# A sliding-window copy on one core: three DMA rings in place of two, new packet sizes, and eleven batches staged in place of twelve

## The chip, the cores and the metric

The kernel runs on one core of a Trainium2 chip. The metric is the device time of one execution in microseconds (us). MB and GB are powers of ten, as in the profile; KB is 1,024 bytes.

## The reference

```
batch, length, dim = (32, 4096, 256); window_size = 64; stride = 32      # float32
n_windows = (length - window_size) // stride + 1                         # 127
for i in range(n_windows):
    start = i * stride
    result[:, i] = x[:, start:start + window_size].copy()
```

Nothing is calculated. Each window is 64 rows of 256 floats, 64 KB without a gap, and the next one begins 32 rows further on. So x falls into blocks of 32 rows (32 KB), 128 to a batch. Window w is blocks w and w+1, and each inner block is written twice: as the second half of one window and as the first half of the next. One batch of x is 4.194 MB; its 127 windows are 8.323 MB of output.

## The kernel before

No compute engine takes part. The work is DMA: an engine's queue issues a transfer, the hardware cuts it into packets, and 16 DMA engines move them. Every issuing queue has a ring of waiting packets on each of the 16. SP feeds q1 and ACT feeds q10 (the bytes in the profile tell which is which). There are two ways for a batch, and the 32 batches are shared out between them:

- **Copied** (20 batches, issued by SP, `copy`, L93). Three transfers go straight from x to the output in memory, of 80, 32 and 15 windows, in packets of 16, 32 and 16 KB (`COPY_PARTS`, L16). The DMA engines move 8.323 MB a batch; memory is read and written for all of it.
- **Staged** (the 12 odd batches 1 to 23, issued by ACT, `load` L75 and `store` L83). One load puts the batch into a tile `xb` of 128 partitions, a block in each (4.194 MB). Two stores write the tile to the first halves of the windows and to the second halves (4.194 MB each). All in packets of 16 KB. The DMA engines move 12.58 MB a batch, and memory is read for one third of that and written for two.

Five tiles are in use in turn (`BUFS`). ACT's program is load 0, load 1, stores 0, load 2, stores 1, and so on (L142 to L148); a store waits for its load (L88), and the load of a tile's next turn waits for both stores of its last (L79). All of these stand one behind the other in one ring.

A store of all 128 blocks writes one block too many at each end: half a window into the batch before and half a window into the batch behind. Those neighbours are copied batches, and they are put right in one of two ways. Most are copied only when the stores that spill into them have landed (L134 to L137; `_order`, L102, places such a batch in SP's list far enough behind). The four of `EARLY` are copied at the very start, and SP writes their spilt halves once more at the end: seven small transfers of 32 KB each, the fringes, in packets of 2 KB (`half`, L46; L152 to L158). ACT waits for the `EARLY` copies before the first store that spills into one (L145 to L147). At the end SP waits for everything and clears 12 semaphores one by one (L159 to L163).

Of the kernel before, what the change touches and what calls it, by code (L numbers as in the profile page):

```python
# [1 line left out]

# [4 lines left out]


STAGED = tuple(range(1, 24, 2))
BUFS = 5  # L10

EARLY = (18, 20, 22, 24)

BLOCK_PARTS = 2

COPY_PARTS = ((80, 4), (32, 2), (15, 4))  # L16


class _Geometry:


    def __init__(self, x, out, W, S):
        self.B, self.L, self.D = x.shape
        self.x, self.out = x, out
        self.n_win = (self.L - W) // S + 1
        self.n_blk = self.L // S
        self.blk = S * self.D
        self.win = W * self.D
        assert W == 2 * S and self.n_blk == self.n_win + 1 == 128

    def src(self, b, block, dims):

        at = (b * self.n_blk + block) * self.blk
        return bass.AP(self.x.tensor, self.x.offset + at, dims)

    def dst(self, b, half, dims):

        at = b * self.n_win * self.win + half * self.blk
        return bass.AP(self.out.tensor, self.out.offset + at, dims)

    def rows(self, b, w0, n):

        s, d = [[self.blk, n], [1, self.win]], [[self.win, n], [1, self.win]]
        return self.dst(b, 2 * w0, d), self.src(b, w0, s)

    def half(self, b, half, block):  # L46

        dims = [[self.blk // 16, 16], [1, self.blk // 16]]
        return self.dst(b, half, dims), self.src(b, block, dims)


class _Kernel:
    def __init__(self, nc, g, tiles):
        self.nc, self.g, self.tiles = nc, g, tiles
        self.loaded = [nc.alloc_semaphore(f"loaded{i}") for i in range(len(tiles))]
        self.stored = [nc.alloc_semaphore(f"stored{i}") for i in range(len(tiles))]
        self.copied = nc.alloc_semaphore("copied")
        self.early = nc.alloc_semaphore("early")
        self.count = {}

    def start(self, engine, out, in_, sem, parts=1):
        engine.dma_start(out=out, in_=in_, max_dma_last_dim=65536 // parts).then_inc(sem, 16)
        self.count[id(sem)] = self.count.get(id(sem), 0) + 16

    def all_of(self, engine, sem):
        engine.wait_ge(sem, self.count[id(sem)])

    def slot(self, n):
        return divmod(n, len(self.tiles))

    def after_store(self, engine, n):
        turn, i = self.slot(n)
        engine.wait_ge(self.stored[i], 32 * (turn + 1))

    def load(self, n):  # L75

        g, (_, i) = self.g, self.slot(n)
        if n >= len(self.tiles):
            self.after_store(self.nc.scalar, n - len(self.tiles))  # L79
        src = g.src(STAGED[n], 0, [[g.blk, g.n_blk], [1, g.blk]])  # L80
        self.start(self.nc.scalar, self.tiles[i][:, :], src, self.loaded[i], 2 * BLOCK_PARTS)

    def store(self, n):  # L83

        g, (turn, i) = self.g, self.slot(n)
        self.nc.scalar.wait_ge(self.loaded[i], 16 * (turn + 1))  # L88
        for half in (0, -1):
            dst = g.dst(STAGED[n], half, [[g.win, g.n_blk], [1, g.blk]])  # L90
            self.start(self.nc.scalar, dst, self.tiles[i][:, :], self.stored[i], 2 * BLOCK_PARTS)

    def copy(self, b, sem):  # L93

        w = 0
        for rows, parts in COPY_PARTS:
            self.start(self.nc.sync, *self.g.rows(b, w, rows), sem, parts)
            w += rows
        assert w == self.g.n_win


def _order(B):  # L102


    near = {b for s in STAGED for b in (s - 1, s + 1)}
    order = list(EARLY) + [b for b in range(B) if b not in near and b not in STAGED]
    tied = sorted(near - set(EARLY))
    n = len(order) + len(tied)
    for b in tied:
        behind = max(STAGED.index(s) for s in (b - 1, b + 1) if s in STAGED)  # L110
        order.insert(-(-(2 * behind + 5) * n // (2 * len(STAGED))), b)
    return order


@with_exitstack
def kernel(
    ctx: ExitStack,
    tc: tile.TileContext,
    x: bass.AP,
    window_size: bass.AP,  # L120
    stride: bass.AP,
    out: bass.AP,
):
    nc = tc.nc
    W, S = int(window_size), int(stride)
    g = _Geometry(x, out, W, S)
    assert 0 not in STAGED and g.B - 1 not in STAGED
    pool = ctx.enter_context(tc.tile_pool(name="blocks", bufs=1))
    tiles = [pool.tile([g.n_blk, g.blk], x.dtype, name=f"xb{i}") for i in range(BUFS)]

    with tc.tile_critical():
        k = _Kernel(nc, g, tiles)
        for b in _order(g.B):
            if b not in EARLY:  # L134
                for s in (b - 1, b + 1):
                    if s in STAGED:
                        k.after_store(nc.sync, STAGED.index(s))  # L137
            k.copy(b, k.early if b in EARLY else k.copied)
        k.load(0)
        waited = False  # L140
        last = len(STAGED) - 1
        for n, s in enumerate(STAGED):  # L142
            if n < last:
                k.load(n + 1)
            if not waited and (s - 1 in EARLY or s + 1 in EARLY):  # L145
                k.all_of(nc.scalar, k.early)
                waited = True  # L147
            k.store(n)  # L148


        k.all_of(nc.sync, k.early)
        for n, s in enumerate(STAGED):  # L152
            if s - 1 in EARLY or s + 1 in EARLY:
                k.after_store(nc.sync, n)
            if s - 1 in EARLY:
                k.start(nc.sync, *g.half(s - 1, 2 * g.n_win - 1, g.n_blk - 1), k.copied)
            if s + 1 in EARLY:
                k.start(nc.sync, *g.half(s + 1, 0, 0), k.copied)  # L158
        for n in range(len(STAGED)):  # L159
            k.after_store(nc.sync, n)  # L160
        k.all_of(nc.sync, k.copied)
        for sem in [*k.loaded, *k.stored, k.copied, k.early]:
            nc.sync.sem_clear(sem)  # L163


# [1 line left out]
_INS = ['x', 'window_size', 'stride']  # L167
_OUTS = [((32, 127, 64, 256), 'float32')]

_NUMBERS = {'window_size': 64, 'stride': 32}  # L170


# [26 lines left out]
```

## Time and profile before

| | |
|---|---|
| median of 3 runs | 763.64 us (762.43 to 763.97) |
| the profiled execution's own time | 768.4 us |
| its span, first to last instruction | 766.6 us |
| moved by the DMA engines | 317.70 MB in 19,837 packets, mean 414 GB/s |
| q1 (SP's ring): the copies and fringes | 10,044 packets, 166.70 MB |
| q10 (ACT's ring): loads and stores | 9,792 packets, 151.00 MB |
| memory read and written | 217.02 and 267.35 MB, 632 GB/s over the span |
| issue to landing, median | 114.8 us (80-window copy), 123.2 us (load), 84.6 us (store) |

How to read it: no engine row has any work but four tiny fills by GpSimd at the start, so the chain of waits between compute engines is empty and tells nothing. What matters is the row of DMA shares over 40 slices (the mean busy share of the 16 DMA engines, in tenths), the row of GB/s below it, and the DMA queues with their packets, bytes and share of 16 engines' time. The same can be asked for any stretch of the span. An issue's time to landing holds its wait in the ring behind all that was issued ahead of it.

### The profile page before, as it was taken

The numbers are of one execution on the slowest core, as the hardware profiler recorded it, in microseconds if no ns is written. First come the engines' busy times: TensorE is split into PE (matmuls) and PEld (weight loads), VectorE is DVE, ScalarE is ACT, GpSimd is POOL, SyncE is SP. The second block draws the span as 40 slices with busy tenths as digits, with TensorE's granted clock in tenths as the row PEclk, the third lists the DMA queues.
The fourth block names the chain that finished last, engine by engine and source line by source line (L and its number), as shares of the span: only waits on it lengthen the run. The fifth ranks groups of instructions, "written<-read, shape, count | busy, mean of one in ns | idle before, by whom it ended". The sixth has DMA issues, their size and how long they took to land. (4 is left out here: it accounts for less than half of the span.)

```text
span 766.6 us, 180 instructions
## 1 busy us (share of the span) xinstructions
POOL 0.2 (0%) x4
## 2 busy tenths in 40 slices
POOL 0000000000000000000000000000000000000000
DMA  8999999999999999999999999999999999999996
GB/s 371 425 410 421 405 428 431 408 411 427 423 415 421 431 415 425 432 408 416 427 420 417 431 420 420 423 428 410 414 427 419 422 428 418 417 428 421 420 406 237
DMA packets 19837, 317.70 MB, mean 414 GB/s; under 512 B 1628, under 2 KB 1628, under 8 KB 1740
## 3 DMA queue, kind: packets, MB, share of 16 engines
q1 hardware_dynamic: 10044, 166.70, 51.9%
q10 hardware_dynamic: 9792, 151.00, 47.3%
q14 instruction: 1, 0.01, 0.0%
HBM read 217.02 MB, written 267.35 MB: 632 GB/s over the span
## 5 line engine op out<-in xcount | busy, mean ns | idle before, releaser
L180 POOL MEMSET const-bfloat16-1.0<- 128x1 bf16 x1 | 0.1, 102 | 0.0
L180 POOL MEMSET const-uint8-127<- 128x1 uint8 x1 | 0.1, 102 | 0.0
L180 POOL MEMSET const-float32-0.0<- 128x1 f32 x1 | 0.1, 99 | 0.2 <-issue 0.2
L180 POOL MEMSET const-float32-1.0<- 128x1 f32 x1 | 0.1, 99 | 0.0
## 6 DMA issues: line engine op xcount, KB each, us to landing
out_dram<-in_x_dram SPq DMA_DIRECT2D x20, 5120.0 KB, 114.8
out_dram<-xb ACTq DMA_DIRECT2D x24, 4096.0 KB, 84.6
xb<-in_x_dram ACTq DMA_DIRECT2D x12, 4096.0 KB, 123.2
out_dram<-in_x_dram SPq DMA_DIRECT2D x20, 2048.0 KB, 116.7
out_dram<-in_x_dram SPq DMA_DIRECT2D x20, 960.0 KB, 97.7
out_dram<-in_x_dram SPq DMA_DIRECT2D x7, 32.0 KB, 48.3
```

The source lines that it names most:

```text
L180: nc = _bacc.Bacc("TRN2", target_bir_lowering=False, num_devices=1)
```

## The change

Eleven odd batches (1 to 21) are staged and 21 are copied; `EARLY` becomes 16, 18, 20, 22. GpSimd issues the loads from load 1 on, on a ring of its own, in packets of 8 KB; ACT keeps load 0 (now without a cut, 32 KB) and issues all stores in packets of 16 KB; SP issues the copies as 112 and 15 windows in packets of 32 KB. The last staged batch is stored in three pieces: partitions 0 to 31, 96 to 127, and then 32 to 95. The first two write what spills into the neighbours and have a semaphore `fringe`, so that the last two fringe transfers wait for those pieces alone. Load 0 has a semaphore `first` of its own. At the end GpSimd, not SP, waits for all semaphores, resets its DMA state and clears the semaphores as one range. There are seven fringe transfers as before.

```diff
-STAGED = tuple(range(1, 24, 2))
+STAGED = tuple(range(1, 22, 2))
-EARLY = (18, 20, 22, 24)
-BLOCK_PARTS = 2
-COPY_PARTS = ((80, 4), (32, 2), (15, 4))
+EARLY = (16, 18, 20, 22)
+LOAD_PACKET = 8192
+STORE_PACKET = 16384
+COPIES = ((112, 2), (15, 2))
+LAST = ((0, 32), (96, 32), (32, 64))
...
     def load(self, n):
         if n >= len(self.tiles):
-            self.after_store(self.nc.scalar, n - len(self.tiles))
+            self.after_store(self.nc.gpsimd, n - len(self.tiles))
         src = g.src(STAGED[n], 0, [[g.blk, g.n_blk], [1, g.blk]])
-        self.start(self.nc.scalar, self.tiles[i][:, :], src, self.loaded[i], 2 * BLOCK_PARTS)
+        if n == 0:
+            self.start(self.nc.scalar, self.tiles[i][:, :], src, self.first)
+        else:
+            self.start(self.nc.gpsimd, self.tiles[i][:, :], src, self.loaded[i], LOAD_PACKET)
...
+    def store(self, n, p0, rows, sem=None):
...
         for half in (0, -1):
-            dst = g.dst(STAGED[n], half, [[g.win, g.n_blk], [1, g.blk]])
-            self.start(self.nc.scalar, dst, self.tiles[i][:, :], self.stored[i], 2 * BLOCK_PARTS)
+            dst = g.dst(STAGED[n], 2 * p0 + half, [[g.win, rows], [1, g.blk]])
+            src = self.tiles[i][p0 : p0 + rows, :]
+            self.start(self.nc.scalar, dst, src, sem or self.stored[i], STORE_PACKET)
...
+        k.load(0)
         for b in _order(g.B):
...
-        k.load(0)
+        for n in range(1, len(STAGED)):
+            k.load(n)
...
-            if n < last:
-                k.load(n + 1)
...
-            k.store(n)
+            if n < last:
+                k.store(n, 0, g.n_blk)
+            else:
+                for p0, rows in LAST:
+                    alone = p0 > 0 and p0 + rows < g.n_blk
+                    k.store(n, p0, rows, None if alone else k.fringe)
...
-            if s - 1 in EARLY or s + 1 in EARLY:
+            if n == last:
+                k.all_of(nc.sync, k.fringe)
+            elif s - 1 in EARLY or s + 1 in EARLY:
                 k.after_store(nc.sync, n)
...
-        for n in range(len(STAGED)):
-            k.after_store(nc.sync, n)
-        k.all_of(nc.sync, k.copied)
-        for sem in [*k.loaded, *k.stored, k.copied, k.early]:
-            nc.sync.sem_clear(sem)
+        sems = [*k.loaded, *k.stored, k.first, k.early, k.copied, k.fringe]
+        for sem in sems:
+            k.all_of(nc.gpsimd, sem)
+        nc.gpsimd.dma_reset()
+        used = sorted(sem.num for sem in sems)
+        nc.gpsimd.sem_clear(range(used[0], used[-1] + 1))
```

## The prediction

> **What bounds the kernel now.** I read the page's DMA rows first, since no compute engine works, then the queues, then single stretches of the span.
>
> ```profile
> DMA  8999999999999999999999999999999999999996
> q1 hardware_dynamic: 10044, 166.70, 51.9%
> q10 hardware_dynamic: 9792, 151.00, 47.3%
> HBM read 217.02 MB, written 267.35 MB: 632 GB/s over the span
> ```
>
> All slices but the first and last are full, and the two rings' shares add up to 99.2% of the time of 16 engines. There is no wait to remove: the time is bytes times what a byte costs a DMA engine. From the rows, per MB on one engine: q1 0.519 x 766.6 us x 16 / 166.70 = 38.2 us, q10 0.473 x 766.6 x 16 / 151.00 = 38.4 us. Straight copies and staged traffic cost the same per byte moved, though a copied byte uses memory twice.
>
> Next, stretches by what ACT's ring is doing. The load that was issued at 44 us is served from 83.5 to 104.6, two stores follow, and so on; three such groups:
>
> ```profile
> 83.50:104.60 21.10, 0.00 (x0) 1.00 1.00 409
> 104.70:125.30 20.60, 0.00 (x0) 1.00 1.01 430
> 125.30:145.70 20.40, 0.00 (x0) 1.00 1.01 427
> 333.80:355.90 22.10, 0.00 (x0) 1.00 1.01 407
> 356.00:376.70 20.70, 0.00 (x0) 1.00 1.02 433
> 376.80:397.20 20.40, 0.00 (x0) 1.00 0.99 418
> 521.80:543.40 21.60, 0.00 (x0) 1.00 1.00 407
> 543.50:563.80 20.30, 0.00 (x0) 1.00 1.00 425
> 563.90:585.00 21.10, 0.00 (x0) 1.00 1.01 421
> ```
>
> Each row ends with the DMA share and GB/s. In the load stretches (first of each three, mean 408) packets take longer than in the store stretches (mean 426), with the engines just as busy: when both rings read memory, something is 4% short. That matters below.
>
> Then how two rings share an engine, from the queues of 31 to 35 us, where most copy packets were the 32 KB ones:
>
> ```profile
> q1 hardware_dynamic: 32, 1.05, 60.7%
> q10 hardware_dynamic: 34, 0.56, 32.5%
> ```
>
> Almost as many packets each, but twice the bytes in q1: the rings take turns packet by packet, so packet sizes set the shares. Last, the end:
>
> ```profile
> 720.00:750.00 30.00, 0.00 (x0) 1.00 0.95 406
> 750.00:753.00 3.00, 0.00 (x0) 1.00 0.91 355
> 753.00:755.00 2.00, 0.00 (x0) 1.00 1.04 393
> 755.00:757.00 2.00, 0.00 (x0) 1.00 0.78 294
> 757.00:759.00 2.00, 0.00 (x0) 1.00 0.78 241
> 759.00:761.00 2.00, 0.00 (x0) 1.00 0.51 198
> 761.00:763.00 2.00, 0.00 (x0) 1.00 0.14 54
> ```
>
> From 720 us the share is 0.95, about 15/16: one engine is out of work. That is the 15-window copy, which can be dealt to 15 engines only. So 15 engines set the end. From 755 us they fall out one by one.
>
> **The change part by part.**
>
> *One staged batch becomes a copied one.* On each of the 15 busy engines a copied batch is 8 windows, 512 KB; a staged one is 256 KB in and 512 KB out. Before: 20 x 512 + 12 x 768 = 19,456 KB. After: 21 x 512 + 11 x 768 = 19,200 KB. The 256 KB (0.262 MB) that go cost 0.262 x 38.3 = **-10.0 us**. All of it is on the path, since nothing else sets the end.
>
> *Packet sizes.* In the trace's packet records the medians are 611 ns for 16 KB and 1,213 ns for 32 KB, so 2 x 611 - 1,213 = 9 ns a packet beyond its bytes; the 4-byte semaphore packets take 9 ns too. Per busy engine before: 20 x (20 + 4 + 4) + 12 x 48 = 1,136 packets. After: copies 21 x 16 = 336, stores 11 x 32 = 352, loads 8 + 10 x 32 = 328, in all 1,016. 120 x 9 ns = **-1.1 us**. An 8 KB packet isn't in the rings of before; by this fit it takes 310 ns. Ends: no saving (0), or this one; what a GpSimd ring could add is a rival below.
>
> *The third ring.* Loads leave ACT's ring. In a full round of turns an engine takes 32 KB of copy, 16 of store, 8 of load: 57, 29 and 14%, where the bytes are 56, 29 and 15%. Load 0 in 32 KB turns ends after 8 rounds of 72 KB, about 22 us at 38.3 us per MB; before, it took 20. Stores of a batch then need 32 rounds, and so does the next load, which has a head start of about 9: ACT's ring doesn't run dry. Loads need tiles: load n waits for stores n-5, four batches back, and queued behind that wait on GpSimd are only later loads, needed later still. SP's list: the last tied batch (14) is 20th of 21 and starts after 19 x 16 rounds, some 650 us; stores 7, for which it waits, land at about 23 + 8 x 68 = 570 us. Issue to landing is 115 us in before, so ahead of that wait SP's ring still holds two copies. The fill of all 16 engines is the cover of all this; if a ring runs dry, the others take its turns, and the cost is only an uneven end.
>
> What the mix does to the rate is the unknown. Before, loads come in lumps of a third of the time with reads only in q10; after, one byte in seven is a load, always. Ends: all of it as in the store stretches, 426 against a mean of 419 over full windows, 1.6% of 750 = -12 us; all as in the load stretches, 408, +2.7% = +20 us. Bytes read from memory as a part of bytes moved are 217.0/317.7 = 68% before, and (174.8 + 46.1 + 0.2)/313.4 = 71% after; it is 100% in the load stretches and about 53% in the others. Linear between those rows, 3 points of 47 times 18 GB/s is 1 GB/s, 0.2%: **+1.5 us**.
>
> *The end.* From 750 us 3.4 MB are left; at 406 GB/s that is 8.5 us, and it took about 13.5. So the end loses 5 us to engines that finish apart and to copies left alone. After, copies run out about 25 store packets an engine (15 us) before the stores, by the count of rounds; the last two fringes wait only for the outer pieces and so are issued before the inner one (16 packets, 10 us) is done. What ends late is then stores, whose stretches were the fast ones. But engines can still finish apart. Ends 0 and -5; I take **-2 us**.
>
> *First and last microseconds.* Load 0 is still ACT's first; only 2 to 6 us was thin (365 GB/s), so at most 1 us either way: 0. SP's 12 clears took 0.7 us (764.9 to 765.6) and become one; GpSimd's reset isn't in the trace. Ends -0.7 and, by the whole stretch behind the last packet, +2.9 once more: 0, as near a clear.
>
> Sum: -10.0 - 1.1 + 1.5 - 2 = -11.6 us. The profiled execution would go from 768.4 to 756.8; it lies 4.8 us over the median of the runs, and I take the same difference from that: 763.64 - 11.6 = **752.0 us**.
>
> A rule that speaks against a third ring: the Trainium skill, "DMA: Bandwidth & Descriptors", section "Rules for kernel authors", says that spreading DMAs over SP, ACT and GpSimd brings no bandwidth, as they use the same 16 engines. The shares of 0.99 to 1.01 above agree that none is idle; by the rule alone the sum is bytes and packets, -11.1 us. The same page, "Queues, rings and completion order", has an engine drain typically 9 to 17 descriptors of a ring before it turns to the next. The 32 against 34 packets above say one at a time for these two rings; if the rule held for GpSimd's ring, loads would take 72 to 136 KB a turn until the tiles are full, which is the fourth rival.
>
> **The rivals.**
>
> 1. *The lumps go* (faster still). Packets are stretched only when everything reads at once. For: 408 against 426. Against: store stretches aren't even themselves (418 to 433). 752 - 1.5 - 12 = **738.5**.
> 2. *The mix is as slow as a load stretch throughout* (slower than before). For: memory traffic per moved byte rises from 484.4/317.7 = 1.52 to 488.5/313.4 = 1.56, and loads are never absent till near the end. Against: 71% of reads is nearer 53 than 100. 752 - 1.5 + 20 = **770.5**. It decides from a full rate of 413 GB/s in the middle (419 less 1.5%).
> 3. *GpSimd's packets are dear* (slower). Its 8 KB load packets are 320 an engine, each with an unknown addition. Low end 0; far end the seven 8 KB packets of the instruction queue, which took 500 ns on average, 190 over the fit: +61 us, **813**. It decides from 11.6 / 0.32 = 36 ns a packet. Those seven are fetches of another kind; the rings' own 9 ns a packet is nearer.
> 4. *The shares don't come out*: loads run ahead, and copies or stores are left alone for long at the end. Bytes are as counted; the end keeps its loss and takes it once more: 752 + 2 + 5 = **759**.
>
> **How the numbers follow.** Forecast (746 to 758) 0.53; rival 1 0.18; rival 4 0.08; rival 2 0.12, of which 0.04 ends within 0.2%; rival 3 0.09, of which 0.01 does. 0.2% (1.5 us) is about what a measurement of this kernel can tell from no change. Faster 0.79, within 0.05, slower 0.16. The range goes down to rival 1's end, 739, and up to 768, which leaves out most of rivals 2 and 3, under 2 in 10.
>
> **What would show it.** A third queue with 42 MB (10 loads), ACT's with about 96, SP's with 175; 313.4 MB in all. Right: 418 to 420 GB/s level through the middle, no dips to 408. Rival 1: over 424. Rival 2: under 413 with the share at 1.0. Rival 3: the third queue's share of time far over its 13% of bytes. Rival 4: a ring that ends over 30 us before the others. The forecast is wrong if the DMA share falls below 0.98 in mid-span.

## The result, and the profile after

The changed kernel takes 753.76 us (median of 6 runs, 751.49 to 756.93) against 763.50 us of the kernel before (median of 6, 761.43 to 764.13). The ratio is 0.9883, with a 95% interval from 0.9856 to 0.9910: faster by 1.2%; by the medians it is 9.7 us. The profiled execution took 756.93 us, the longest of the six, with a span of 755.1. The profiled execution of before took 768.4, 4.8 us above the median, so a second trace of before (e11) stands beside it below.

From the page of the changed kernel, the DMA queues and the memory row:

```profile
q1 hardware_dynamic: 6209, 175.02, 54.8%
q10 hardware_dynamic: 6192, 96.47, 30.4%
q0 software_dynamic: 5280, 41.94, 13.6%
HBM read 221.15 MB, written 267.29 MB: 647 GB/s over the span
```

A third queue, q0, is GpSimd's, with the ten loads. Its share of time, 13.6%, is about its share of the bytes, 41.94 of 313.43 MB or 13.4%. The shares still add up to 98.8%: the engines are as full as before, with 4.27 MB less to move.

The queues from 300 to 340 us of the changed kernel (packets, MB, share of 16 engines):

```profile
q1 hardware_dynamic: 316, 9.34, 55.9%
q10 hardware_dynamic: 317, 4.93, 29.6%
q0 software_dynamic: 317, 2.47, 15.2%
```

One packet of each ring in turn, GpSimd's too, so the bytes go 56 to 29 to 15, as the sizes 32, 16 and 8 KB say (the semaphore packets are counted too).

Stretches of the changed kernel (the last two columns are the DMA share and GB/s):

```profile
150.00:600.00 450.00, 3.70 (x5) 1.00 1.01 423
690.00:705.00 15.00, 0.00 (x0) 1.00 0.98 393
744.00:746.00 2.00, 0.00 (x0) 1.00 0.71 296
746.00:748.00 2.00, 0.00 (x0) 1.00 0.40 166
```

The middle is level at 423 GB/s. When the loads are through, at about 668 us, the rate falls, and from 690 us on it is below 400 though the engines are still nearly full. From 744 us the engines fall out one by one, as in before.

The same stretch of before in its second trace (e11), and then one load stretch and the store stretch behind it:

```profile
150.00:600.00 450.00, 0.00 (x0) 1.00 1.01 424
331.50:353.60 22.10, 0.00 (x0) 1.00 1.01 403
353.70:374.10 20.40, 0.00 (x0) 1.00 1.01 430
```

So the mean rate in the middle hardly changed, 424 (420 in the first trace of before) against 423. What changed is how much had to be moved at it. The question left is why fewer bytes came at the same rate, and whether the third ring has a part in that.

### The profile page after: what moved, and what is told of

It reads as the page before. It is cut to its first block, busy times and chain, and to the rows that moved or that the text cites. A ratio compares the mean times of both kernels' runs of the same rounds, so it can differ in the third digit from the quotient of the medians.

```text
span 755.1 us, 155 instructions
## 1 busy us (share of the span) xinstructions
POOL 7.7 (1%) x14
## 2 busy tenths in 40 slices
DMA packets 17681, 313.43 MB, mean 415 GB/s; under 512 B 1355, under 2 KB 1355, under 8 KB 1467
## 3 DMA queue, kind: packets, MB, share of 16 engines
q0 software_dynamic: 5280, 41.94, 13.6%
## 4 chain that ended last, share of the span: by engine, by line
another core or an unknown queue 58%; POOL 1%; issue 0%; PEldq 0%
POOL xb L68 1%; PEldq L217 0%
## 5 line engine op out<-in xcount | busy, mean ns | idle before, releaser
L68 POOL DMA_DIRECT2D xb<-in_x_dram x10 | 7.5, 754 | 439.8 <-DMA out_dram<-xb 438.8
```

Source lines behind the costliest of these rows:

```text
L68: engine.dma_start(out=out, in_=in_, max_dma_last_dim=packet).then_inc(sem, 16)
```

## The experiments

Three theories. **Bytes**: only the KB on the busy engines count; the third ring is an ornament. **Rings**: the third ring and its packets make the gain. **Memory**: time goes with what memory reads and writes. Out of the first results came a fourth, the **roof**: the rate is the smaller of two limits, what the engines can move and what memory can read and write together. Traffic below means reads and writes of memory added up: 2 for a copied byte, 1 for a loaded or stored one.

### e1: two rings, eleven batches staged

```diff
 # the kernel before
-STAGED = tuple(range(1, 24, 2))
-EARLY = (18, 20, 22, 24)
-COPY_PARTS = ((80, 4), (32, 2), (15, 4))
+STAGED = tuple(range(1, 22, 2))
+EARLY = (16, 18, 20, 22)
+COPY_PARTS = ((48, 4), (64, 2), (15, 4))
```

> The kernel before with eleven batches staged and the copies cut 48 windows in 16 KB, 64 in 32 KB, 15 in 16 KB, so that both rings still end together (504 copy packets and 528 staged ones an engine); two rings, 16 KB loads on ACT's ring as before. Theory of bytes (the gain is the 256 KB fewer on each of 15 engines): -10 us for the bytes and -1 for 104 fewer packets, 752.5 us, as fast as the changed kernel. Theory of rings (the gain comes from the loads' own ring, which spreads the reads): 760 us or more.

Measured: 761.84 us, ratio to before 0.9985 (0.9976 to 0.9993). The same 313.4 MB as the changed kernel, and almost nothing gained. Its middle:

```profile
150.00:600.00 450.00, 0.00 (x0) 1.00 1.01 420
```

About 1% below before, and later slower too (600 to 700 us: 417 against 422): here a byte cost more. Bytes alone (752.5 us) are refuted; 760 or more is what the theory of rings gave.

### e8: the same with the old cut of the copies

> The kernel before with eleven batches staged and nothing else changed: 588 copy packets against 528 staged ones an engine, so copies are left alone for the last 60 packets, about 1,100 KB or 42 us. Bytes -10; copies alone cost 12% of 42 us, +5: 758.5 us. If balance of the rings doesn't matter: 753 us.

Only STAGED and EARLY of e1's edit. Measured: 765.56 us, ratio 1.0030 (1.0018 to 1.0041), slower than before. The middle holds 424 GB/s (300 to 450 us), but ACT's ring is through early, and the copies alone from 700 us on move 332 GB/s (700 to 730 us). The balance of the rings matters, more than was expected: copies alone cost 28% more than this kernel's own middle (332 against 424), not 12%. Over 42 us that is 12 us, so -10 and +12 make +2, where +2.3 was measured.

### e2 and e9: three rings, twelve batches staged

```diff
 # the changed kernel; e2
-STAGED = tuple(range(1, 22, 2))
-EARLY = (16, 18, 20, 22)
+STAGED = tuple(range(1, 24, 2))
+EARLY = (18, 20, 22, 24)
 # e9 has this as well
-LAST = ((0, 32), (96, 32), (32, 64))
+LAST = ((0, 128),)
```

> The changed kernel with twelve batches staged, as before. Theory of bytes: 19,456 KB an engine again, -0.6 us for 72 fewer packets than before, -2 for the end: 761 us. Theory of rings: 753 us. Theory of memory (time goes with what memory reads and writes, 484 MB here against 488 in the changed kernel): 748 us.

> e2 (three rings, twelve batches staged) with the last batch stored in one piece. In e2 the stores that ran alone at the end moved 258 to 273 GB/s from 735 to 750 us, while the two pieces of 32 partitions were in the ring. If reading 32 partitions is what slows them: 20 us at some 265 and 334 instead of 400 GB/s are 6 us, so 760.5 us. If stores alone are slow however they are cut: 766 us. Theory of a roof (the rate is the smaller of 430 GB/s by the engines and 665 GB/s of memory traffic): 317.7 MB at 430 against 313.4 at 665/1.559 = 427, +5 us from the changed kernel with a whole last store (752.6): 757.5 us.

Measured: e2 766.92 us, ratio 1.0053 (1.0039 to 1.0067); e9 760.16 us, ratio 0.9963 (0.9950 to 0.9977). In both, the stores are left alone at the end. Two stretches of e2, when the two pieces of 32 partitions are in the ring, and then one of e9, where stores are alone too:

```profile
735.00:740.00 5.00, 0.00 (x0) 1.00 0.96 265
740.00:745.00 5.00, 0.00 (x0) 1.00 1.00 258
```

```profile
730.00:740.00 10.00, 0.00 (x0) 1.00 1.01 431
```

Stores alone run at the engines' full rate; pieces of few partitions don't, and cost e2 6.8 us (766.92 - 760.16, on two chips whose medians of before differ by 0.2). e9 is the clean one: with before's bytes, the change of rings is worth 2.9 us (763.08 - 760.16). That is a bundle: the third ring, all packet sizes, and the shorter clears at the end, and no run takes it apart. e9 comes near what the theory of bytes gave for e2 (761 us); those of rings (753) and of memory (748) fall, and the roof's figure for e9 (757.5) is 2.7 us low.

### e3, e5 and e6: fewer batches staged, down to none

e3 and e5 change STAGED and EARLY alone: `range(1, 20, 2)` with (14, 16, 18, 20), and `range(1, 16, 2)` with (10, 12, 14, 16). e6 is only SP's loop:

```diff
 # the changed kernel; e6
+        for b in range(g.B):
+            k.copy(b, k.copied)
+        k.all_of(nc.sync, k.copied)
```

> The changed kernel with ten batches staged. Theory of bytes: 256 KB fewer an engine, -10 us from 753.8, and copies left alone at the end for about 22 packets an engine, 27 us at 12% more as copies alone took at the end of the kernel before, +3: 747 us. Theory of memory: 492.6 MB against 488.4, +0.9%: 760 us.

> The changed kernel with eight batches staged; copies are left alone at the end. Theory of bytes: 18,432 KB an engine, -30 us from 753.8, and about 118 copy packets of 32 KB alone, 145 us at 12% more, +17: 741 us. Theory of memory (500.8 MB against 488.4): 773 us.

> All 32 batches copied straight on SP's ring in 32 KB packets; no tile, no staging. 16,384 KB on each busy engine, the least bytes there can be. Theory of bytes, with the 12% that copies alone cost at the end of the kernel before: about 625 x 1.12 + 5 = 705 us. Theory of memory (532.7 MB against 488.4 in 753.8 us): 822 us.

Measured: e3 756.31 us, ratio 0.9915 (0.9900 to 0.9931); e5 766.19, ratio 1.0037 (1.0025 to 1.0048); e6 807.14, ratio 1.0570 (1.0549 to 1.0591). Neither theory's numbers hold: each result lies between them. The pages say why. e6's memory row, then two late stretches of e3, when first the loads and then the stores are through:

```profile
HBM read 266.34 MB, written 266.34 MB: 662 GB/s over the span
```

```profile
600.00:700.00 100.00, 0.00 (x0) 1.00 1.00 398
700.00:730.00 30.00, 0.00 (x0) 1.00 0.95 335
```

Copies alone read and write each byte: 334 GB/s in mid-span of e6 (300 to 700 us) are 668 of traffic. In the first stretch of e3, 27.25 of the 39.80 MB are copies, which is 1.685 of traffic a byte: 398 x 1.685 = 671. And three rings, by the queues' MB from 300 to 340 us of the changed kernel, (2 x 9.34 + 4.93 + 2.47) / 16.74 = 1.558: 423 x 1.558 = 659. Three mixes, within 2% of one number: memory gives this core about 666 GB/s, reads and writes together. The engines give about 430. Which of them binds depends on the mix.

A rival is that each engine is slow at copying by itself, whatever memory gives. The end of e6, where engines run out of work, answers it. With 16 engines busy, with 15, and with 12 (shares 1.00, 0.94 and 0.75):

```profile
300.00:700.00 400.00, 0.00 (x0) 1.00 1.00 334
712.00:780.00 68.00, 0.00 (x0) 1.00 0.94 332
788.00:800.00 12.00, 0.00 (x0) 1.00 0.75 325
```

The total stays nearly the same, and what a packet takes changes: 32 KB took 1,554 ns at the median from 300 to 700 us, and every one of the last stretch 1,213 ns, the median of the kernel before. So the limit is one that the engines share.

### e7: loads in packets of 32 KB

```diff
-LOAD_PACKET = 8192
+LOAD_PACKET = 32768
```

> The changed kernel with GpSimd's loads in packets of 32 KB in place of 8, so that they take 40% of the turns' bytes until the tiles are full, and come in lumps. If the ratio of packet sizes matters: stretches of 408 GB/s come back and the rings end apart, 760 us. If only bytes matter: 240 packets fewer an engine, -2 us, 752 us.

Measured: 767.49 us, ratio 1.0050 (1.0030 to 1.0070); 13.7 us over the changed kernel by the medians, for one constant. The loads now run ahead until the tiles are full and then pause. A stretch with loads, and one where they have ended:

```profile
195.00:225.00 30.00, 0.00 (x0) 1.00 1.00 425
540.00:640.00 100.00, 0.00 (x0) 1.00 1.00 405
```

While loads take their large turns the traffic is (64 + 16 + 32) / 80 = 1.4 a byte by the packet sizes, and the rate is near the engines' limit. Without loads 26.54 of 40.53 MB are copies, 1.655 a byte, and memory binds, at 405 x 1.655 = 670. Time under one limit isn't given back under the other: from 150 to 600 us e7 moves 413 GB/s in the mean, the changed kernel 423, which is 11 us. What the third ring brings depends on its packet size.

### e4: the last batch stored whole

```diff
-LAST = ((0, 32), (96, 32), (32, 64))
+LAST = ((0, 128),)
```

> The changed kernel with the last batch stored in one piece, so that the last two fringe transfers wait for the last store. If the split is worth something: two transfers of 32 KB behind the last store, issue to landing some 3 us: 757 us. If the uneven end of the engines covers it: 754 us.

Measured: 752.57 us (752.18 to 753.51), ratio 0.9868 (0.9856 to 0.9881). The pieces bring nothing; the changed kernel's interval overlaps, so that they cost something here, where copies still run beside them, is not shown. e4 is the fastest version of the study, by median.

### e10 and e12: the mixes one at a time

```diff
 # e10; tiles 0 to 4; each stage waits for the last; K = 16384
+        stage("loads", [(load, i, i, K) for i in range(5)], [])
+        stage("stores", [(store, i, 1 + 2 * i, K) for i in range(5)], [])
+        stage("loadcopy", [(load, i, 5 + i, K) for i in range(5)], [(copy, 20 + i, K) for i in range(3)])
+        stage("storecopy", [(store, i, 1 + 2 * i, K) for i in range(5)], [(copy, 20 + i, K) for i in range(6)])
+        stage("narrow", [(narrow, i, 1 + 2 * i, K) for i in range(5)], [])
+        stage("loadstore", [(load, i, 10 + i, K) for i in range(2)], [(store, 3, 1, K)])
 # e12, behind the same loads
+        stage("loadcopy32", [(load, i, 5 + i, K) for i in range(5)], [(copy, 20 + i, 2 * K) for i in range(6)])
+        stage("storecopy32", [(store, i, 1 + 2 * i, K) for i in range(5)], [(copy, 20 + i, 2 * K) for i in range(11)])
+        stage("loadparts", [(load, i, 5 + i, K) for i in range(5)], [(parts, 20 + i) for i in range(3)])
+        stage("storeparts", [(store, i, 1 + 2 * i, K) for i in range(5)], [(parts, 20 + i) for i in range(6)])
```

> Not the reference's work: stages one behind the other, each waiting for the last, all in 16 KB packets, with part of the output left unwritten. Loads alone on ACT's ring; stores alone on ACT's; loads on ACT's beside copies on SP's; stores on ACT's beside copies on SP's; stores of partitions 0 to 31 alone; loads on ACT's beside stores on SP's. Theory of a roof (430 GB/s moved, 665 GB/s of memory traffic, whichever is less, reads and writes alike): loads 430, stores 430, loads beside copies 430, stores beside copies 430, loads beside stores 430. Theory of read lumps (memory does less where nearly all is read): loads beside copies 405 to 410, stores beside copies 425 to 430. Pieces of 32 partitions: 265 if few partitions are slow, 430 if not.

> Not the reference's work: stages one behind the other, with part of the output left unwritten; loads and stores on ACT's ring in 16 KB packets. Loads alone; loads beside copies of 112 windows in 32 KB packets; stores beside the same; loads beside copies cut as before (80, 32 and 15 windows, 16, 32 and 16 KB); stores beside the same. Theory of a roof (the smaller of 430 GB/s moved and 666 GB/s of memory traffic): with 32 KB copies 1.667 bytes of traffic a byte, 400 GB/s beside loads and beside stores alike; cut as before 430 while packets are 16 KB and 400 in the 32 KB fifth, 424 in all, beside loads and beside stores alike. Theory that reads and writes count apart: loads beside copies of either kind well below stores beside the same, 408 against 426 for the old cut.

`load`, `store` and `copy` are single transfers as in the kernel, with the packet size as last argument (`copy` of 112 windows); `narrow` stores partitions 0 to 31 of each tile; `parts` copies a batch in the old cut. Measured, the middle of the first five stages of e10 in their order:

```profile
6.00:48.00 42.00, 0.00 (x0) 1.00 1.01 430
60.00:145.00 85.00, 0.00 (x0) 1.00 1.00 427
160.00:245.00 85.00, 0.00 (x0) 1.00 1.01 432
265.00:440.00 175.00, 0.00 (x0) 1.00 1.01 432
465.00:505.00 40.00, 0.00 (x0) 1.00 1.02 210
```

The sixth stage, loads beside stores, moved 428 GB/s. Then the four stages of e12 behind its loads:

```profile
65.00:195.00 130.00, 0.00 (x0) 1.00 1.00 394
230.00:510.00 280.00, 0.00 (x0) 1.00 1.00 404
545.00:620.00 75.00, 0.00 (x0) 1.00 1.01 431
655.00:830.00 175.00, 0.00 (x0) 1.00 1.01 430
```

Loads, stores, and either beside copies of equal packets (1.5 of traffic a byte): 427 to 432, the engines' limit. Either beside copies of twice the packet (1.667): 394 and 404, which is 657 and 673 of traffic, memory's limit. Whether the other ring reads or writes makes 2.5%; how much of the mix is copies makes more. Few partitions are slower still than in e2, 210 where 265 was expected.

For the old cut of the copies the roof failed as it was worked out, packet size by packet size: 424 was expected and 431 and 430 came, beside loads and beside stores. Counted over the whole stretch the traffic is 1.52 a byte, and 666 / 1.52 = 438 is above what the engines give, so the engines bind. And loads beside this cut don't show the dip that the load stretches of before had.

### e11: before again

> The kernel before, unchanged, for a second trace beside the changed kernel's, since its profiled execution lay 4.8 us over its median. Bytes theory and roof theory alike: 763 us, with the load stretches at 408 GB/s and the store stretches at 426 again.

Measured: 762.46 us. Load stretches (403 to 415 GB/s) and store stretches (425 to 436) stand as far apart as in the first trace. Here are a load without its end, its end with the passage to the stores behind it, and those stores:

```profile
331.50:350.00 18.50, 0.00 (x0) 1.00 1.00 413
350.00:354.00 4.00, 0.00 (x0) 1.00 1.00 352
354.00:374.00 20.00, 0.00 (x0) 1.00 1.01 432
```

Over all ten loads of e11 that have stores on both sides, the last 4 us of a load moved 385 GB/s and the 4 us behind it 410, the load ahead of that 423, and the rest of the two stores 429. In the first trace it was 395, 416, 416 and 426. So the stores run near the engines' limit, and what before loses it loses at its loads: in e11 some 70% of that, in the first trace half, in the 8 us where ACT's ring passes from a load to stores.

## Why the prediction was right, step by step

The forecast was 752.0 us, the result 753.76; -11.6 us were expected and -9.7 came. The runs divide the gain as 2.9 us for the rings with before's bytes (e9) and 7.6 for the batch that is copied in place of staged (e9 to e4), with some 1.2 lost again by the pieces of the last store, a step within the noise. The sum fits; its terms only in part.

- **What bounds the kernel.** Right that the engines are full and no wait counts. Incomplete: a full engine isn't one at its own limit. Its packets are stretched when memory can't follow, and the page shows that as busy time: in mid-span of e6 the share is 1.00 while a 32 KB packet takes 1,554 ns at the median, not 1,213. The step "straight copies and staged traffic cost the same per byte" was read from two rings that run together: each is stretched by the mix they make. Copies alone cost 1.3 times as much (334 against 430 GB/s). (The load stretch at 83.5 us is, by the order in the ring, the load issued at 21.8 us, not at 44; its rate is read rightly.)
- **-10.0 us for 256 KB an engine.** With three rings, from twelve staged batches to eleven (e9 to e4, the whole last store in both), -7.6 us. With two rings -1.1 (e1), or +2.3 (e8). The bytes are on the path, but they are saved by swapping staged for copied, which needs more memory traffic for each byte. The price of 38.3 us per MB came near only where the mix stayed level.
- **-1.1 us for fewer packets.** Not tested alone. GpSimd's 8 KB packets took 309 ns at the median of the trace's packet records, against 310 by the fit, so the third rival (dear packets) falls.
- **+1.5 us for the mix.** The size fits, by luck: 423 against 424 GB/s in the middle is 0.2%. The reason given, the share of reads, falls: e10 has loads beside copies at 432. Two different losses came out nearly equal. Before loses at its loads, while its stores run at 426 to 429, near the engines' limit. The changed kernel has no lumps of loads, but its level mix of 1.558 takes 659 GB/s of traffic, close to memory's limit (666 / 1.558 = 427), and its copy packets of 32 KB are stretched a little, to 1,236 ns in the mean from 150 to 600 us. That memory does this stretching is worked out from the mixes, not shown by a run of its own. With before's bytes and three rings the middle moved 426 (e9), with the change's bytes 425 (e4): so the extra copying cost little there.
- **-2 us for the end.** Not borne out. The split of the last store, on which it leaned, brings nothing (e4), and the engines fall out one by one as before. Behind 668 us, when the loads are through, 32 KB copies beside 16 KB stores run into memory's limit, which the prediction missed. Counted from 600 us on, against what the same bytes would take at the kernel's own middle rate, the end costs 8.4 and 8.5 us in the two traces of before, 12.2 in the changed kernel and 10.4 in e4: 2 to 4 us more, not 2 less.
- **0 for the first and last microseconds.** About right: the first packet starts at 1.9 to 2.0 us in all four traces, and behind the last one 2.8 us became 2.3 (1.8 in e4).
- **The rivals.** The first (the lumps go, 738.5) had a part: the slow load stretches did go, but the level mix then met memory's limit, and the rate came to 423, not 426. The second (the mix as slow as a load stretch throughout, 770.5) named memory's traffic, with the wrong price: by 666 / 430 memory binds from about 1.55 of traffic a byte, an estimate, and the changed kernel stands just there. e3 and e5 spend their last part beyond it. The fourth (the shares don't come out) is e7, with 13.7 us where 7 were put down.

Open: why ACT's ring is slow where it passes from a load to stores, and why the rest of the load stretches of before was slow too in its first trace (416). By traffic load and store stretches are alike, and apart from the rest loads beside the same copies run at 431 (e12). Open too: why e1 moved 420 in its middle. Its queues make 1.56 of traffic a byte there, as in the changed kernel; its loads come in lumps as in before, but no run tests that.

The rule that spreading DMAs over three issuers brings no bandwidth (the Trainium skill, "DMA: Bandwidth & Descriptors", section "Rules for kernel authors") is right here in that no engine had time to spare. But at equal bytes the third ring with its packet sizes was worth 2.9 us (e9); that it did so by ending the lumps of loads is argued from the traces. The same page's 9 to 17 descriptors a turn, in "Queues, rings and completion order", doesn't hold for these packets: all three rings gave one a turn (316, 317 and 317 packets in 40 us).

## What to carry to other kernels

This kernel had two limits: about 430 GB/s moved by the engines, and about 666 GB/s that memory reads and writes. In a kernel bound by DMA, count both for each stretch, and look for the mix at which they meet. A full busy row doesn't tell which one binds: compare a packet's duration with that of the same packet where nothing else runs. The rings took turns packet by packet here, so packet sizes set the mix; keep it level over time and let the rings end together, because time under one limit wasn't returned under the other (e7, e8).

## What the runs showed of the hardware that had not been expected

- Memory traffic of one core, reads and writes together, levelled off at 657 to 673 GB/s in every copy-rich mix; loads or stores alone moved 427 to 430 GB/s, straight copies 334. Twelve engines copy about as much as sixteen (325 against 334, e6).
- Stores that read partitions 0 to 31 alone moved 210 GB/s (e10), half of 427, with all engines shown as busy; 258 to 265 at the end of e2.
- Repeated runs of the changed kernel spread over 5.4 us (751.49 to 756.93), those of before over 2.7; the whole last store's spread over 1.3. The cause is open.
